# Two contraction tiles instead of one between the short products, in the projections of a three-block transformer kernel

## The chip, the cores and the metric

The kernel runs on one core of one Trainium2 chip. The metric is the device time of one execution in microseconds (us). A core has TensorE (PE in the profile; its weight loads are PEld), VectorE (DVE), ScalarE (ACT), GpSimd (POOL) and SyncE (SP), which here issues most DMAs. Each engine works through its own list of instructions in the order in which the program wrote them.

## The reference, cut to what matters

One batch of 512 tokens, 1024 wide, in float32, goes through two blocks of a first model and one of a second. The change touches the middle one, the gated delta rule, and the last one.

```python
def first_block(x, ...):
    for i in range(2):                                  # block 0: attention, block 1: delta rule
        h = rms_norm(x); mem_n = rms_norm(mem)
        mixed = attention(h, mem_n) if i == 0 else deltanet(h, mem_n)
        x = x + rms_norm(mixed)
        x = x + rms_norm(swiglu(rms_norm(x)))
    return x

def deltanet(h, mem_n):                                 # 6 heads of 128, chunks of 64 tokens
    qkv, z, gate_in, q_mem = split(h @ w_in)            # the projections
    q, k, v = split(silu(conv5(qkv)))                   # q, k are normalised per head
    g, beta = gates(gate_in)                            # for both directions
    o = chunked(q, k, v, g[0], beta[0]) + reversed(chunked)(q, k, v, g[1], beta[1])
    o = rms_norm(o) * out_norm * silu(z)
    return concat([o, memory_attention(q_mem, mem_n)]) @ w_out

def chunked(q, k, v, g, beta):
    # per chunk: solve (I + strict(beta k k^T decay)) [u, w] = [beta v, beta k exp(g)]
    # then, chunk after chunk:
    v_new = u - w @ state
    out = (q * exp(g)) @ state + intra @ v_new
    state = state * exp(g_last) + (k * exp(g_last - g))^T @ v_new

def second_block(x):
    proj = rmsnorm(x) @ w_in                            # the projections again
    mix = concat([gla(proj), s5(proj), nsa(proj)])      # three mixers
    return x + mix @ w_out
```

## The kernel before, in words

**Products.** Every large product is taken in three passes: an operand is split into a high part and a rest, and `mm3` (lines 267 to 269) multiplies rest by high, high by rest, high by high into one PSUM bank. The normalised activations stand transposed in `Xh` and `Xl`: eight contraction tiles of 128 features by 512 tokens. Weights are fetched by SP into `raw` (three buffers), ACT makes the high part `wh` (line 239), DVE the rest `wl` (line 258); four split pieces fit at a time (the set `wsl`).

**Who sets the order.** The program is written by a planner, `Flow`. The parts of the work are generators ("threads") that ask for an engine with an estimated cost, for a buffer from a named set, or for an event. `Flow.run` takes the request that could start first by its own clock; among those of the same engine that could start within 0.1 us of it, it takes the one with the lowest `late` number. So the lists of all engines come out of these estimates; an engine then waits at run time for whatever its next instruction needs. What stands on TensorE between two dependent short products was put there by the planner.

**The projections' thread.** `projector` is used twice: for the delta stage (called in `deltanet`, with the default `late=20`) and for the second block. It goes through weight pieces in a fixed order. A piece of 128 output features is one item; its product is written by `part`, which asks for TensorE once per contraction tile `k` and then writes that tile's three passes. Eight requests make one item, 24 passes (the first four items are taken in two halves of 256 tokens). Items that are lists of pieces (the token-major ones of the second block) have a loop of their own with one request per three passes. In the delta stage the pieces are the gates, then key, query, value of each head, the memory's two query pieces, and z, the output gate, of which heads 3 to 5 stand at the end. When all are written, the event `eP` lets the thread `splits` overwrite `Xh` and `Xl` with the finished heads (lines 1696 and 1698), and the next product begins: the delta block's output projection in `tok_proj`, with the head outputs stationary and `w_out` moving (in the profile `bk<-wh,Xl`, where the projections are `bk<-Xh,wl`). Its first group takes three token tiles through the contraction tiles 6, 7, 0, 1, 2, 3, 4, 5, three passes per token tile and contraction tile: 63 passes that don't need head 5, then 9 that do.

**The short products of a head**, each a thread with a low `late`:
- `key`, `query`, `value`: convolution on DVE (line 1290), transposes (line 1301: `pk`, `pq`, `pv`), `kk` and `kq`;
- `inverse`: transposes of the decayed matrix (line 1469), then five rounds of `x` (line 1502), a transpose `tt` (1483), copies on ACT, `y` (1521), and a predicated copy into `U` on DVE (1526); a last round (1539, 1559) whose results DVE scales into `Uf` (1563);
- `chain`, one per direction, both side by side, four chunks each: `chain<-rhs,Uf` (line 1594), a copy `vn` on ACT (1597), `vs` on DVE (1602), `chain<-vs,ktok` (1604), the new state `St` on DVE (1608 or 1611), `chain<-St,kTh` (1586), `rhs` on DVE (1589), and again; beside it the outputs `o` (1616, 1617);
- `gate_out`: squares on ACT (1641), a power and a multiplication on POOL (1318, 1648), the transpose `poT` (line 1301), and the gated result `oT` on DVE (1651), which `splits` then splits for the output projection.

Of the kernel before, what the change touches and what calls it, by code (L numbers as in the profile page):

```python
# [35 lines left out]
S = 512  # L36
D = 1024
KT = D // P
# [120 lines left out]
class K:  # L159
# [1618 lines left out]
    def projector(self, F, items, eX, eP, late=20, haste=0):  # L1778

        X = self.X
        yield "late", late

        def part(it, t0, t1):
            W, m = it["W"], it["args"][4]
            yield "wait", *eX[t0 // P:t1 // P]  # L1790
            for k in range(KT):
                t = yield "PE", 0.65 * (t1 - t0) / S
                self.mm3(it["p"][:m, t0:t1], (W.h[:, k, :], W.l[:, k, :]), (X.h[:, k, t0:t1], X.l[:, k, t0:t1]),
                         k == 0, k == KT - 1)
            if t1 == S:
                F.put("wsl", t)
                it["done"]["tok"] = t
            return t
        lent = ["px", "lv"]
        for nm in lent:  # L1800
            yield "move", nm, "mm"
        for t0, t1 in ((0, 256), (256, S)):
            for it in items[:4]:
                if not t0:
                    yield "get", "mm"
                    it["p"] = self.psum("mm")
                    yield "wait", it
                t = yield from part(it, t0, t1)
        for i, it in enumerate(items):
            if i < 4:  # L1810
                continue
            if i == len(items) - haste:
                yield "late", -0.5
            if lent:
                yield "move", "mm", lent.pop()
            if isinstance(it, dict):
                yield "wait", it
                yield "get", "mm"
                it["p"] = self.psum("mm")
                t = yield from part(it, 0, S)  # L1820
                continue
            yield "wait", *it, it[0]["use"]
            for u in range(4):
                yield "wait", eX[u]
                yield "get", "mm"
                p = self.psum("mm")
                sl = slice(u * P, (u + 1) * P)
                for k in range(KT):
                    W, kk = it[k // 4]["W"], k % 4
                    t = yield "PE", 0.33  # L1830
                    self.mm3(p[:, :256], (X.h[:, k, sl], X.l[:, k, sl]), (W.h[:, kk, :], W.l[:, kk, :]),
                             k == 0, k == KT - 1)
                evac, late_ = it[0]["use"]["f"]
                F.add(evac(u, p), late_, t)
            for _ in range(2):
                F.put("wsl", t)
        eP["tok"] = t
# [1447 lines left out]
```

## Time and profile before

| what | value |
|---|---|
| three runs of the kernel | 1831.49, 1836.02, 1836.78 us; median 1836.02 |
| the profiled execution | 1834.01 us, span of its profile 1832.3 us |
| TensorE busy | 97% of the span, 12127 matmuls |
| mean granted TensorE clock | 0.991 of full speed |
| chain that ended last | PE 88%, DVE 7%, issue 2%, ACT, DMA, POOL 1% each |

The profile is one execution with every instruction's start and duration. The page gives busy time per engine. The windows view gives it per stretch, with the granted TensorE clock as a share of full speed (1.00 is the level of 2.4 GHz, 0.50 that of 1.2 GHz). The timeline gives single instructions; a matmul's duration there contains its way through the pipeline, so that the distance between two starts, not the duration, is what it costs on a busy TensorE. An entry in square brackets is idle time of the engine just before the instruction, and what ended it.

Places in time: the delta stage's first transposes stand at 708 us, its last projection at 1028 us, `poT` of head 5 at 1054 us; the second block's projections run from 1488 us.

### The profile page before, as it was taken

What the parts mean: (1) busy time and instruction counts of PE and PEld (TensorE: products, weight loads), DVE (VectorE), ACT (ScalarE), POOL (GpSimd) and SP (SyncE); (2) the same over time, 40 slices, a digit from 0 to 9 for tenths busy, and PEclk for the clock granted to TensorE, in tenths of its full rate; (3) what the DMA queues carried; (4) which work ended last, traced back from release to release, by engine and by line L of the source; (5) the groups of instructions that cost most, each with busy time, mean ns of one, the idle gap of its engine ahead of it and who ended that gap; (6) DMA issues with size and microseconds to landing.
All of it is one profiled execution on the core that took longest, in us unless ns stands there. A gap on an engine that the chain in (4) does not pass through costs nothing.

```text
span 1832.3 us, 30457 instructions
## 1 busy us (share of the span) xinstructions
PE 1782.6 (97%) x12127; PEld 1488.2 (81%) x12127; DVE 977.5 (53%) x1997; ACT 769.7 (42%) x1848; POOL 337.3 (18%) x496
## 2 busy tenths in 40 slices
PE   6999999999999999999999989999999999999999
PEld 5988888888888887787878778888888888887787
DVE  6333366423333378775876456454533566466673
ACT  5433445332322245655655445333222352344671
POOL 5200001000000021221222153175450032210000
PEclk8999999999999999999999999999999999999999
DMA  6511113433233233111110155345333252552112
GB/s 187 149 58 49 55 59 127 138 92 103 93 92 104 92 115 81 42 30 36 36 36 25 47 130 137 116 137 145 98 111 102 74 164 80 157 145 67 36 36 81
DMA packets 213006, 167.85 MB, mean 92 GB/s; under 512 B 21996, under 2 KB 185084, under 8 KB 212864
## 3 DMA queue, kind: packets, MB, share of 16 engines
q1 hardware_dynamic: 204832, 154.39, 28.5%
q0 software_dynamic: 4560, 9.42, 2.0%
q10 hardware_dynamic: 3472, 2.10, 0.4%
q8 instruction: 95, 1.56, 0.4%
q14 instruction: 47, 0.39, 0.1%
HBM read 152.23 MB, written 13.65 MB: 91 GB/s over the span
## 4 chain that ended last, share of the span: by engine, by line
PE 88%; DVE 7%; issue 2%; ACT 1%; DMA 1%; POOL 1%; ACTq 0%; SPq 0%; DVEq 0%; POOLq 0%
PE bk L267 23%; PE bk L268 22%; PE bk L269 22%; PE x L1502 2%; PE y L1521 2%; PE no L2739 1%; DVE hn L1290 1%; DVE wl L258 1%; PE npT L2722 1%; PE gs L2095 1%; PE tt L1483 1%; PE ms_s L825 1%; DVE hs L908 1%; PE as L627 1%; PE ns L2708 1%
## 5 line engine op out<-in xcount | busy, mean ns | idle before, releaser
L258 DVE TENSOR_TENSOR wl<-raw,wh 128x512 fp32r<-128x512 f32 x450 | 315.7, 742 | 369.4 <-ACT wh L239 368.7
L239 ACT ACTIVATE wh<-raw 128x512 fp32r<-128x512 f32 x474 | 272.7, 622 | 539.1 <-PE bk L269 304.3
L267 PE MATMUL bk<-Xh,wl 128*128 128x512 f32 (+2 forms) x1312 | 495.0, 377 | 0.2 <-ACT Xh L917 0.2
L268 PE MATMUL bk<-Xl,wh 128*128 128x512 f32 (+2 forms) x1312 | 478.4, 365 | 0.5 <-DVE Xl L922 0.3
L269 PE MATMUL bk<-Xh,wh 128*128 128x512 f32 (+2 forms) x1312 | 478.4, 365 | 0.0
L267 PEld LDWEIGHTS bk<-Xh,wl 128*128 128x128 f32 (+1 forms) x1312 | 247.2, 188 | 41.2 <-issue 5.0
L269 PEld LDWEIGHTS bk<-Xh,wh 128*128 128x128 f32 (+1 forms) x1312 | 247.0, 188 | 40.1
L268 PEld LDWEIGHTS bk<-Xl,wh 128*128 128x128 f32 (+1 forms) x1312 | 247.5, 189 | 34.8 <-DVE Xl L922 0.9
L267 PE MATMUL bk<-wh,Xl 128*128 128x256 f32 (+1 forms) x456 | 167.4, 367 | 6.0 <-ACT wh L239 4.3
L268 PE MATMUL bk<-wl,Xh 128*128 128x256 f32 (+1 forms) x456 | 158.4, 347 | 0.1
L269 PE MATMUL bk<-wh,Xh 128*128 128x256 f32 (+1 forms) x456 | 158.2, 347 | 0.0
L267 PE MATMUL bk<-wh,Al 128*128 128x512 f32 x352 | 139.8, 397 | 0.0
L268 PE MATMUL bk<-wl,Ah 128*128 128x512 f32 x352 | 139.6, 396 | 0.0
L269 PE MATMUL bk<-wh,Ah 128*128 128x512 f32 x352 | 138.6, 394 | 0.0
L887 POOL TENSOR_TENSOR nc<-ncm,nhalf 128x1 f32<-128x1 f32 x16 | 11.6, 723 | 690.1 <-DVE ncm L885 686.0
L267 PEld LDWEIGHTS bk<-wh,Xl 128*128 128x128 f32 x456 | 96.0, 211 | 20.1 <-ACT wh L239 4.7
L269 PEld LDWEIGHTS bk<-wh,Xh 128*128 128x128 f32 x456 | 96.4, 211 | 7.9
L268 PEld LDWEIGHTS bk<-wl,Xh 128*128 128x128 f32 x456 | 96.5, 212 | 7.5 <-DVE wl L258 1.0
L1059 DVE TENSOR_TENSOR sg<-sg,bk 128x512 f32<-128x512 f32 x44 | 30.3, 688 | 124.4 <-PE bk L269 119.9
L269 PEld LDWEIGHTS bk<-wh,Ah 128*128 128x128 f32 x352 | 66.1, 188 | 16.0
L267 PEld LDWEIGHTS bk<-wh,Al 128*128 128x128 f32 x352 | 66.1, 188 | 16.0
L268 PEld LDWEIGHTS bk<-wl,Ah 128*128 128x128 f32 x352 | 66.1, 188 | 15.4
(588 smaller groups left out, 2678.3 us busy)
## 6 DMA issues: line engine op xcount, KB each, us to landing
raw<-in_ffn_w_gate_up_dram SPq DMA_DIRECT2D x88, 512.0 KB, 3.9
raw<-in_ffn_w_down_dram SPq DMA_DIRECT2D x44, 512.0 KB, 3.3
raw<-in_dn_w_in_dram SPq DMA_DIRECT2D x27, 512.0 KB, 3.7
raw<-in_att_w_in_dram SPq DMA_DIRECT2D x20, 512.0 KB, 3.7
raw<-in_w_in_dram SPq DMA_DIRECT2D x20, 512.0 KB, 4.2
raw<-in_mem_w_kv_dram SPq DMA_DIRECT2D x8, 512.0 KB, 3.7
raw<-in_att_w_out_dram SPq DMA_DIRECT2D x8, 512.0 KB, 3.3
xd<-x SPq DMA_DIRECT2D x8, 512.0 KB, 3.2
```

What stands on the lines that cost most here:

```text
L239: nc.scalar.activation(wh[:, sl], ev["raw"][:, sl], AF.Copy)
L258: eng.tensor_tensor(wl[:, sl], raw[:, sl], wh[:, sl].bitcast(F32), op=OP.subtract)
L267: mm(out, A[1], B[0], start=first, stop=False, **kw)
L268: mm(out, A[0], B[1], start=False, stop=False, **kw)
L269: mm(out, A[0], B[0], start=False, stop=last, **kw)
L627: nc.tensor.matmul(s[:, c, lo:hi], qT[rr, c, ts], kT[rr, c, k0 + lo:k0 + hi], start=True, stop=True)
L825: nc.tensor.matmul(s[:, c, :], q[rr, c, ts], self.memK[i][rr, c, :], start=True, stop=True)
L908: nc.vector.scalar_tensor_tensor(hh[:, hv[i]], x[:, t, hv[i]], r2, r["gain"][:, hv[i]], op0=OP.mult, op1=OP.mult)
L1059: nc.vector.tensor_tensor(sg, sg, pu, op=OP.mult)
L1290: nc.vector.scalar_tensor_tensor(acc[:, d0:d1], raw[:, d0 + o:d1 + o], cw[:, ti, tap:tap + 1], acc[:, d0:d1], op0=OP.mult, op1=OP.add)
L1502: nc.tensor.matmul(dn8(x)[HB[c % 2], d, c // 2, :], Ln[d][HB[f], c, HB[f]], U[HB[f], d, c, :], start=True, stop=True)
L1521: nc.tensor.matmul(dn8(y)[HB[f], d, n, :], T[HB[par], d, n, f, :], xs[f][HB[par], d, n, :], start=True, stop=True)
```

## The change

In `part`, one request now covers two contraction tiles, at twice the estimated cost, and writes six passes. Nothing is added or removed; the planner then orders the instructions of all engines anew. Line numbers above 1788 grow by one.

```diff
         def part(it, t0, t1):
             W, m = it["W"], it["args"][4]
             yield "wait", *eX[t0 // P:t1 // P]
-            for k in range(KT):
-                t = yield "PE", 0.65 * (t1 - t0) / S
-                self.mm3(it["p"][:m, t0:t1], (W.h[:, k, :], W.l[:, k, :]), (X.h[:, k, t0:t1], X.l[:, k, t0:t1]),
-                         k == 0, k == KT - 1)
+            for k0 in range(0, KT, 2):
+                t = yield "PE", 1.3 * (t1 - t0) / S
+                for k in (k0, k0 + 1):
+                    self.mm3(it["p"][:m, t0:t1], (W.h[:, k, :], W.l[:, k, :]), (X.h[:, k, t0:t1], X.l[:, k, t0:t1]),
+                             k == 0, k == KT - 1)
             if t1 == S:
                 F.put("wsl", t)
                 it["done"]["tok"] = t
```

**TensorE, the short products of head 0 early in the delta stage** (transposes `pq` and `pkT`, then the rows of the decay). The piece of the difference:

```order
 L268 MATMUL bk<-Xl,wh 128x512
 L269 MATMUL bk<-Xh,wh 128x512
+L267 MATMUL bk<-Xh,wl 128x512
+L268 MATMUL bk<-Xl,wh 128x512
+L269 MATMUL bk<-Xh,wh 128x512
 L1301 MATMUL pq<-ident,qTh 128x128 x4
-L267 MATMUL bk<-Xh,wl 128x512
-L268 MATMUL bk<-Xl,wh 128x512
-L269 MATMUL bk<-Xh,wh 128x512
 L1301 MATMUL pkT<-ident,ktok 128x128 x4
```

Three passes that stood between the two transposes have joined the burst ahead of them, and the transposes now stand side by side.

**TensorE, the end of head 4's inverse** (its last `y`) and the start of its chain. Before:

```order
L1559 MATMUL y_9214<-xs_9152,T 64x64 x4
L267 MATMUL bk<-Xh,wl 128x512
L268 MATMUL bk<-Xl,wh 128x512
L269 MATMUL bk<-Xh,wh 128x512
L1411 MATMUL kq<-qTh,kTh 128x128 x4
L1594 MATMUL chain<-vtok,Uf 128x128
L267 MATMUL bk<-Xh,wl 128x512
```

Now:

```order
L269 MATMUL bk<-Xh,wh 128x512
L1559 MATMUL y_9385<-xs_9327,T 64x64 x4
L1594 MATMUL chain<-vtok,Uf 128x128 x2
L1604 MATMUL chain<-vs_9409,ktok 128x128
L1604 MATMUL chain<-vs_9412,ktok 128x128
L1617 MATMUL o<-vn_9405,AT_8426 128x128
L1469 MATMUL y_9423<-ident,Ln_9224 128x128 x4
L1586 MATMUL chain<-St_9419,kTh 128x128
```

The last pass of the delta stage's 528 now stands ahead of head 4's last `y`; before, 72 passes still followed the chain's first product. Nothing stands any more between that `y`, the chain's first product and its second.

**TensorE, the end of head 5's chain, up to `poT`.** Before (between the last of these rows and `poT` follow the other `o` products and 24 passes of the output projection):

```order
L1586 MATMUL chain<-St_9935,kTh 128x128
L1586 MATMUL chain<-St_9940,kTh 128x128
L267 MATMUL bk<-wh,Xl 128x512
L268 MATMUL bk<-wl,Xh 128x512
L269 MATMUL bk<-wh,Xh 128x512
L1594 MATMUL chain<-rhs_9949,Uf 128x128
L1594 MATMUL chain<-rhs_9954,Uf 128x128
L267 MATMUL bk<-wh,Xl 128x512
L268 MATMUL bk<-wl,Xh 128x512
L269 MATMUL bk<-wh,Xh 128x512
L1616 MATMUL o<-St_9935,qe_9011 128x128
L1617 MATMUL o<-vn_9958,AT_8972 128x128
```

Now:

```order
L1586 MATMUL chain<-St_9974,kTh 128x128
L1586 MATMUL chain<-St_9979,kTh 128x128
L1594 MATMUL chain<-rhs_9988,Uf 128x128
L1594 MATMUL chain<-rhs_9990,Uf 128x128
L1616 MATMUL o<-St_9974,qe_9165 128x128
L1617 MATMUL o<-vn_9994,AT_9146 128x128
L1616 MATMUL o<-St_9979,qe_9345 128x128
L1617 MATMUL o<-vn_9996,AT_9319 128x128
L1301 MATMUL poT<-ident,otok 128x128 x4
L267 MATMUL bk<-wh,Xl 128x512
```

No pass of the output projection stands between head 5's first chain product and its `poT` any more: all 63 that don't need head 5 stand ahead of it (54 stood ahead of `poT` before), and the first pass behind `poT` is one that does need head 5.

Counted in the two orders from the first transpose of line 1301 in the delta stage to `poT` of head 5, the passes come in 116 bursts before (75 of three, 25 of six, 16 longer) and in 93 now (10 of three, 76 of six, 7 longer).

## Rows read from the trace of the kernel before

**Rows 1.** The page: busy time per engine, share of the span, instructions.

```profile
PE 1782.6 (97%) x12127; PEld 1488.2 (81%) x12127; DVE 977.5 (53%) x1997; ACT 769.7 (42%) x1848; POOL 337.3 (18%) x496
```

**Rows 2.** Windows: stretch, length, busy us (PE, PEld, DVE, ACT, POOL), PE clock, DMA.

```profile
708.00:1028.00 320.00, 313.09 (x3544) 255.91 (x3544) 224.32 (x512) 174.95 (x500) 68.95 (x57) 0.99 0.13 38
1028.00:1056.90 28.90, 25.75 (x153) 21.61 (x151) 15.33 (x40) 10.60 (x32) 6.45 (x9) 0.94 0.11 37
...
1490.00:1690.00 200.00, 195.82 (x1700) 167.38 (x1700) 118.36 (x270) 81.02 (x188) 39.22 (x44) 0.99 0.44 120
```

**Rows 3.** Timeline of TensorE, one burst of six: start, duration, instruction.

```profile
742.26 0.48 PE L267 MATMUL bk<-Xh,wl 128*128 128x512 f32 x1
742.58 0.40 PE L268 MATMUL bk<-Xl,wh 128*128 128x512 f32 x1
...
743.50 0.39 PE L269 MATMUL bk<-Xh,wh 128*128 128x512 f32 x1
743.82 0.97 PE L1521 MATMUL y<-xs,T 64*64 64x64 f32 x32
```

**Rows 4.** TensorE's waits, 708 to 1060 us: total, times, longest.

```profile
PE chain L1604 <- DVE vs L1602: 2.8, 2, 1.6
PE chain L1594 <- DVE Uf L1563: 2.1, 2, 1.7
PE x L1502 <- DVE U L1526: 1.8, 1, 1.8
PE x L1502 <- DVE U L1472: 1.2, 1, 1.2
```

**Rows 5.** Timeline of TensorE in head 5's chain and behind it.

```profile
1033.57 1.05 PE L1604 MATMUL chain<-vs,ktok 128*128 128x128 f32 x4
...
1037.90 0.60 PE L1594 MATMUL chain<-rhs,Uf 128*128 128x128 f32 x4
...
1039.72 0.61 PE L1604 MATMUL chain<-vs,ktok 128*128 128x128 f32 x4
1040.09 0.48 PE L267 MATMUL bk<-wh,Xl 128*128 128x512 f32 x1
...
1041.75 0.61 PE L1586 MATMUL chain<-St,kTh 128*128 128x128 f32 x4
...
1042.90 0.60 PE L1594 MATMUL chain<-rhs,Uf 128*128 128x128 f32 x4
...
1048.42 0.39 PE L1617 MATMUL o<-vn,AT 128*128 128x128 f32 x2
...
1054.11 0.60 PE L1301 MATMUL poT<-ident,otok 128*128 128x128 f32 x4
...
1056.94 0.50 PE L267 MATMUL bk<-wh,Xl 128*128 128x512 f32 x1 [0.17 <-DVE Xl L1698]
```

**Rows 6.** Timeline of DVE and POOL in the same stretch.

```profile
1038.68 0.51 DVE L1602 TENSOR_SCALAR vs<-vn,ksc 128x128 f32<-128x128 f32 x2 [0.30 <-ACT vn L1597]
1039.43 0.69 DVE L1698 TENSOR_TENSOR Xl<-oT,Xh 128x512 fp32r<-128x512 f32 x1 [0.23 <-ACT Xh L1696]
1040.14 0.60 DVE L1608 SCALAR_TENSOR_TENSOR St<-St,etot,chain 128x128 f32<-128x128 f32 x2
...
1042.18 0.61 DVE L1589 SCALAR_TENSOR_TENSOR rhs<-chain,neg,vtok 128x128 f32<-128x128 f32 x2 [0.83 <-PE chain L1586]
...
1052.08 1.04 POOL L1648 TENSOR_TENSOR otok<-otok,rro 128x512 f32<-128x512 f32 x1
```

**Rows 7.** Windows around two stretches with waits, same columns.

```profile
733.00:745.00 12.00, 9.06 (x160) 7.59 (x160) 11.72 (x24) 9.09 (x19) 3.45 (x3) 1.00 0.17 45
...
1073.00:1078.00 5.00, 4.90 (x11) 3.60 (x12) 2.12 (x5) 1.25 (x4) 0.00 (x0) 0.51 0.57 151
```

**Rows 8.** TensorE's two longest waits, 1490 to 1832 us.

```profile
PE ncs L2649 <- DVE Q L2617: 2.0, 2, 1.6
PE nqT L2609 <- DVE nqd L2604: 1.9, 1, 1.9
```

## The prediction

> **What bounds the kernel now.** I read the page first: TensorE is busy for 1782.6 us of the span [rows 1], so what can be won or lost is its idle time and the price of its busy time. The windows give the idle time by stage [rows 2]: 320.00 - 313.09 = 6.9 us between the first transposes of the delta stage and its last projection, 28.90 - 25.75 = 3.15 us from there to the first product that needs head 5's result, 4.2 us in the second block's projections. The stages ahead of the delta stage aren't touched; in the second feed-forward the order stays as it is. The view of waits names what ended the idle time: always DVE, with a result of a head's convolution, inverse or chain that came late [rows 4]. The timeline then shows the price of the bursts [rows 3] and, at the end of the delta stage, the steps of a chain with and without passes between them [rows 5, 6].
>
> **The change part by part.** No instruction comes or goes, no DMA moves past another one of its queue. What counts is where passes stand.
>
> *Bursts.* Inside a burst a pass costs 0.23 us ((743.50 - 742.58) / 4). The first one costs 0.32 (742.26 to 742.58), and the last one 0.32 up to the short product behind it [rows 3]. So a burst costs 0.18 us beyond its passes. The delta stage has 93 in place of 116. Where a burst goes, two short products meet and have an edge of their own, so I take three quarters: 23 x 0.13 = **-3.0 us** (bounds 0 and 23 x 0.18 = -4.1). The second block has as many bursts as before.
> The Trainium skill says on the page "TensorE: Matmul & The Clock Gate", section "Step-by-step: what each phase is for", that TensorE pulls weight loads ahead of matmuls in flight, so that the next tile's weights load while this one runs. By that rule changing over would be free and this term 0; the trace doesn't agree, with 0.32 against 0.23 at both ends of the burst.
>
> *Waits in the body of the delta stage.* 6.9 us, most of it in four waits of 1.2 to 1.8 us, two of the inverse and two of the chain [rows 2, 4]. Where a dependent short product follows a burst, the burst is now three passes longer and hides 0.7 us more; where a burst has gone, it hides 0.7 less. DVE's own order is new too, and which of its results comes late can't be read. I take **-2.0 us**: 0.7 of three of the four waits. Bounds: -6.9 (all hidden) and +3 (the four places at which a burst has gone from behind a short product, 0.7 each).
>
> *The end of the delta stage.* Twice the passes go into each gap, so the projections are used up earlier, ahead of head 4's chain. From there the planner fills gaps from the output projection, three passes at a time, and all 63 that it may take are used up before head 5's chain begins. That chain had a burst at nearly every step and has none now. Its steps cost:
> - chain product to `vs` to next product: from 1037.90 to the first half of `vs` (1038.68 + 0.26) and 0.1 to start: 1.1 us [rows 5, 6]. TensorE's own four instructions fill 0.37 (1039.72 to 1040.09); 0.73 is idle.
> - `chain<-St` to `rhs` to next product: 1041.75 to 1042.18 + 0.30 and 0.07: 0.80, less 0.37: 0.43 idle.
> - in between, the state `St` (1039.72 to 1040.14 + 0.30) is hidden by the output products.
> - three chunks: 3 x (0.73 + 0.43) = 3.5; the last chunk 0.2; the wait for `Uf` at the start 0.5 (2.1 for two of them where DVE was busy with other work [rows 4]).
> - the last `o` to `poT`: squares, power, multiplication end at 1052.08 + 1.04 = 1053.12, 4.7 us after 1048.42; less 0.2 of its own: 4.5 idle. 24 passes hid this before.
> - `poT` to the first pass with head 5: 1054.11 to 1056.94, 2.83, less 0.37: 2.45 idle. Nine passes hid it but for 0.17.
>
> Together 3.5 + 0.2 + 0.5 + 4.5 + 2.45 = 11.15, less the 3.15 that this stretch idled before: **+8.0 us**. Bounds +5 (the steps that pair up hide each other) and +11.
>
> *Head 4's chain* starts without cover for its first two steps: 0.5 + 0.73. The seven splits for the output projection (0.69 each on DVE [rows 6]) now fall between its steps in place of head 5's. Fully exposed they are 4.8; about 2 should show, since bursts of three still stand at half of the steps. **+3.2 us** (bounds +1.2 and +6.0).
>
> *The clock.* After the wait that ends at 1073 us, 11 passes took 4.90 us at a granted clock of 0.51 [rows 7], 0.445 each in place of 0.23: 2.4 lost. The idle time around `poT` should bring the same. Before, the chain's first round ran slowly too: 1033.57 to 1037.90 is 4.33, the next round 3.18 with two more pairs of output products (0.4) [rows 5]; so 1.6 lost goes. Net **+0.8 us**. Bounds -1.6 and +5.
>
> *The second block.* Its two longest waits, 1.9 and 2.0 us [rows 8], have more ahead of them now: 39 passes of half width where 27 stood (12 x 0.12 = 1.4) and 12 of full width where 9 stood (0.7). **-2.0 us**; bounds -4 (both gone) and +3 (four steps of the last mixer without a burst of three).
>
> The stall at 1073 us is a chain of its own from the first pass with head 5 to weights that are fetched when a buffer comes free, and moves along with it: 0.
>
> Sum: -3.0 - 2.0 + 8.0 + 3.2 + 0.8 - 2.0 = **+5.0 us** on the profiled execution's 1834.0. The median of the three runs shown is 2.0 above that execution, so I put the time at 1836.0 + 5.0 = **1841.0 us**.
>
> **The rivals.**
> *The tail runs at 1.2 GHz.* For: head 5's chain idles 1.16 of some 3.2 us in each chunk, and after the waits around 1029 to 1033 us the chain's round was slow [rows 5]. Against: the stretch from 733 to 745 us idled 3 of 12 us and kept a clock of 1.00 [rows 7]. It decides where the idle share lies between these two. The price: three groups of 0.37 in a chunk take twice as long, 1.1, for four chunks of head 5 and perhaps one of head 4: 5.5 us. Time 1841.0 + 5.5 = 1846.5.
> The Trainium skill has the same page's section "What's actually happening" for it: "the default state is throttled, and activity releases the throttle"; by that rule sparse small products are what brings the lower level back. The two stretches just named show both outcomes.
>
> *The waits on DVE vanish* (not slower). Place: the waits of the body and the two of the second block, all for results of DVE that were a little late. If the longer bursts hide all of them and head 4 shows its bare 1.2, the sum is -3.0 - 6.9 + 8.0 + 1.2 + 0.8 - 4.0 = -3.9: 1832.1. It needs two bursts' worth of extra cover (1.4 us) at most of these places. For: each wait is below 1.9 us. Against: DVE was busy for 11.72 of 12 us at the first of them [rows 7], so that there its own work sets the time.
>
> *Changing over is free*, as the rule on weight loads has it: the sum without -3.0 is +8.0, 1844.0. Rows 3 speak against it.
>
> That the change doesn't do what it says is excluded: the new order has 76 bursts of six.
>
> **How the numbers follow.** About 0.3%, 5.5 us, is what a measurement of this kernel can tell from no change: below 1830.5 is faster, above 1841.5 slower. My sum lies just at the upper edge. Forecast: 0.49, of which 0.25 slower and 0.24 within. Tail at the low clock: 0.20, all slower. Waits vanish: 0.25, of which 0.12 faster and 0.13 within. Free changes: 0.06, of which 0.05 slower. So slower 0.50, same 0.38, faster 0.12. The range takes in both rivals' times and the larger bounds of the tail: 1830 to 1850. Sums above 0.3% and sums within it share most of the chance but sit beside each other; the forecast's own range is 1835 to 1847.
>
> **What would show it.** The profile of the changed kernel should show TensorE idle for 9 to 14 us between the last projection of the delta stage and the first pass with head 5 (3.15 before), among it one wait of 4 to 5 us ahead of `poT`, ended by POOL, and one of about 2.4 behind it, ended by DVE's split; a granted clock of 0.5 after them; below 6.9 us of idle time in the body; and the two waits of the second block shorter by 1 us or so each. I am wrong if the gap ahead of `poT` is missing, if the body's idle time grows, or if the second block's last mixer, which I left out but for a bound, begins to wait.

## The result, and the profile after

The changed kernel took 1850.96 us (median of five runs, 1846.61 to 1855.85), the kernel before 1835.06 us beside it (1831.49 to 1836.78): a ratio of 1.0088, 95% interval 1.0075 to 1.0101. It is slower, as forecast, but by 15.9 us in place of 5.0, and just outside the range. The profiled execution is the one of 1846.61 us, 12.6 above that of before.

The page's engine line of the changed kernel answers to [rows 1]: the same 12127 matmuls, 9.2 us more of busy time.

```profile
PE 1791.8 (97%) x12127; PEld 1493.8 (81%) x12127; DVE 979.1 (53%) x1997; ACT 767.9 (42%) x1848; POOL 338.0 (18%) x496
```

Windows of the changed kernel, columns as in [rows 2]: the delta stage to its last projection, head 4's chain, head 5's chain to the first pass that needs it; then, in the second block, 3.9 us of short products and what followed them.

```profile
707.00:1003.70 296.70, 289.93 (x3094) 238.37 (x3095) 210.10 (x471) 162.36 (x462) 63.03 (x51) 0.99 0.14 40
1003.70:1047.00 43.30, 41.96 (x527) 34.13 (x525) 19.94 (x53) 16.40 (x48) 6.02 (x7) 0.96 0.04 14
1047.00:1067.40 20.40, 11.71 (x81) 9.65 (x75) 8.61 (x28) 5.01 (x21) 5.44 (x8) 0.87 0.08 27
...
1532.70:1536.60 3.90, 3.90 (x56) 3.63 (x54) 1.69 (x5) 0.63 (x1) 0.51 (x1) 1.00 0.16 32
...
1536.60:1550.30 13.70, 13.70 (x82) 11.11 (x81) 5.24 (x13) 3.09 (x6) 3.29 (x7) 0.50 0.33 99
```

The last two lines are the surprise. TensorE is busy all the time, no wait stands ahead, and for 13.7 us the granted clock is 0.50. The kernel before ran the same short products, and much the same passes behind them, at 1.00, as its windows show:

```profile
1527.70:1531.35 3.65, 3.65 (x54) 3.38 (x53) 1.55 (x5) 0.63 (x1) 0.30 (x1) 1.00 0.12 18
1531.35:1544.00 12.65, 12.65 (x136) 10.29 (x135) 7.52 (x20) 3.47 (x7) 3.50 (x7) 1.00 0.39 108
```

TensorE's waits in the changed kernel, 707 to 1070 us and then 1490 to 1844 us (total, times, longest); they answer to [rows 4, 8]. The wait ahead of `poT` is there, and a wait of the second block that before did not have: `s5y`, a product of the S5 mixer, for its state `q` from DVE. The wait for `npT`, in the block's last mixer, was 0.3 us before.

```profile
PE pk L1301 <- DVE kraw L1271: 5.1, 2, 3.8
PE poT L1301 <- POOL otok L1648: 4.4, 1, 4.4
PE mo L864 <- DVE mpT L854: 2.5, 1, 2.5
PE chain L1604 <- DVE vs L1602: 2.5, 4, 1.1
PE bk L267 <- DVE Xl L1698: 2.2, 1, 2.2
...
PE nqT L2610 <- DVE nqd L2605: 3.1, 2, 1.8
PE npT L2723 <- ACT nP L2715: 1.4, 2, 1.1
PE s5y L2333 <- DVE q L2314: 1.4, 1, 1.4
```

TensorE's timeline in head 5's chain, changed kernel; it answers to [rows 5].

```profile
1047.86 0.61 PE L1594 MATMUL chain<-vtok,Uf 128*128 128x128 f32 x4
1048.93 0.71 PE L1604 MATMUL chain<-vs,ktok 128*128 128x128 f32 x4 [0.47 <-DVE vs L1602]
...
1050.76 0.75 PE L1594 MATMUL chain<-rhs,Uf 128*128 128x128 f32 x4 [0.22 <-DVE rhs L1589]
...
1064.06 1.12 PE L1301 MATMUL poT<-ident,otok 128*128 128x128 f32 x4 [4.36 <-POOL otok L1648]
1067.41 0.80 PE L267 MATMUL bk<-wh,Xl 128*128 128x512 f32 x1 [2.23 <-DVE Xl L1698]
```

### The profile page after: what moved, and what is told of

It is laid out like the page before. It is cut to its first block, busy times and chain, and to the rows that moved or that the text cites. A ratio compares the mean times of both kernels' runs of the same rounds, so it can differ in the third digit from the quotient of the medians.

```text
span 1844.9 us, 30450 instructions
## 1 busy us (share of the span) xinstructions
PE 1791.8 (97%) x12127; PEld 1493.8 (81%) x12127; DVE 979.1 (53%) x1997; ACT 767.9 (42%) x1848; POOL 338.0 (18%) x496
## 4 chain that ended last, share of the span: by engine, by line
PE 88%; DVE 7%; ACT 2%; issue 2%; POOL 1%; DMA 1%; ACTq 0%; DVEq 0%; POOLq 0%
PE bk L267 23%; PE bk L268 22%; PE bk L269 22%; PE y L1521 1%; PE x L1502 1%; DVE wl L258 1%; PE no L2740 1%; DVE hn L1290 1%; PE npT L2723 1%; PE gs L2096 1%; PE ms_s L825 1%; PE tt L1483 1%; PE as L627 1%; DVE hs L908 1%; PE hT L915 1%
## 5 line engine op out<-in xcount | busy, mean ns | idle before, releaser
L258 DVE TENSOR_TENSOR wl<-raw,wh 128x512 fp32r<-128x512 f32 x450 | 320.3, 753 | 363.9 <-ACT wh L239 363.2
```

Of the source, the lines that this page charges most:

```text
L258: eng.tensor_tensor(wl[:, sl], raw[:, sl], wh[:, sl].bitcast(F32), op=OP.subtract)
```

## The experiments

They ran on three chips (e1 to e4, e5 to e8, e9 to e12), each time beside the kernel before, whose median was 1833.95, 1835.77 and 1834.96 us there; each ratio is to that. All start from the kernel before, with the number of contraction tiles per request as a parameter `n` of `projector`, a function of the item's place (27 items in the delta stage):

```diff
+            for k0 in range(0, KT, n):
+                t = yield "PE", 0.65 * n * (t1 - t0) / S
+                for k in range(k0, k0 + n):
+                    self.mm3(...)
```

### One block at a time

The delta stage alone (e1, the first pair of lines), the second block alone (e2, the second pair):

```diff
-        F.add(self.projector(F, order, eX, eP))
+        F.add(self.projector(F, order, eX, eP, n=lambda i: 2))
...
-        F.add(self.projector(F, W["order"], eX, eAll, haste=1))
+        F.add(self.projector(F, W["order"], eX, eAll, haste=1, n=lambda i: 2))
```

> Two tiles per request in the delta stage only; the second block keeps one. Theory A (the cost is the delta stage's end: no passes left between the steps of head 5's chain, plus the low clock behind it; in the second block's first mixers the changed kernel's profile fell to the low clock by chance of where the clock's decision fell, not by its order): about +7 us against the kernel before, 1842. Theory B (each block's new order costs in its own place): also about +7 here, so this run alone doesn't tell them apart; its sum with the next one does. Theory C (the longer bursts cost nothing by themselves, all of it is the low clock): the same idle time as before at the end of the delta stage and a lower clock.

> Two tiles per request in the second block only. Theory A: within 3 us of the kernel before on average, 1833 to 1838, with the profile either free of a low-clock stretch around the first mixers or with one that the kernel before can have too. Theory B: +6 to +8 us, 1841 to 1843, and the low-clock stretch of some 14 us around the first mixers is there again.

Measured: e1 1840.24 us, ratio 1.0035 (1.0018 to 1.0052), 12 runs from 1834.1 to 1848.8; e2 1836.06 us, ratio 1.0004 (0.9985 to 1.0022), 12 runs from 1834.12 to 1844.72. The halves don't add: +0.35% and +0.04% against +0.88% for both. Theory A's forecasts came nearly (+6.3 and +2.1 us), theory B's +6 to +8 for e2 did not; but then about half of what the change costs stands in neither half. e2's profile (1844.11 us) shows the low clock too: 20.5 us at 0.50 from 1558.1 us on, behind a wait of 1.40 us for `q`. And runs of one kernel differ by up to 15 us, with a mean clock of 0.984 in the longest and 0.995 in the shortest. Even the kernel before does that: of the 29 runs shared by this and the next section, 21 lie from 1830.6 to 1835.7 and eight from 1837.9 to 1844.9. So something that comes in some executions alone is at work, and more often with the change: nine of its eleven runs (five above, six of e4 below) took 1846.6 us or more.

### Two tiles for the first heads alone, and the change once more

```diff
+        F.add(self.projector(F, order, eX, eP, n=lambda i: 2 if i < 15 else 1))
```

This leaves 36 passes of the output projection beside head 5's chain (54 before, none in the change). The second block is that of before.

> Two tiles per request in the delta stage for the first 15 pieces (gates, heads 0 to 2, memory) and one for the other 12 (heads 3 to 5 and their z). 36 passes of the output projection then stand between the steps of head 5's chain and poT, where the kernel before has 54 and the changed one none, but only 3 of them behind the last o, where the kernel before has 24. Theory A: the chain's own steps are covered, the wait ahead of poT stays at 3.5 to 4 us: +3 us against the kernel before, 1838. Theory B: about as much as with two tiles in the whole delta stage, +7.

> The changed kernel once more, for a second trace. Theory A: the wait ahead of poT (4.4 us) and behind it (2.2 us) stand in it again; the low-clock stretch around the first mixers of the second block may be missing or lie elsewhere, and the time of the profiled execution then differs from the first one's by about 6 us. Theory B: the stretch is there again, of the same length. Median 1847 to 1853 by both.

Measured: e3 1835.06 us, ratio 0.9995 (0.9975 to 1.0015), in two groups, 1827.4 to 1832.8 and 1837.3 to 1841.1; e4 1850.89 us, ratio 1.0084 (1.0051 to 1.0118), from 1840.6 to 1859.4. e3 can't be told from the kernel before, so the forecasts of both theories (+3 and +7) missed. The profile of e3 fell into its upper group, and its windows show the low clock at the same place, for longer, though its second block is in the order of before:

```profile
1525.10:1528.80 3.70, 3.70 (x55) 3.43 (x53) 1.60 (x5) 0.63 (x1) 0.32 (x1) 1.00 0.13 21
1528.80:1552.70 23.90, 23.90 (x148) 18.92 (x149) 7.88 (x21) 3.47 (x7) 3.48 (x7) 0.50 0.30 91
```

Half of 23.9 us would be 12 us; from the first to the last `gs` product it is 75.2 us here and 64.6 in the kernel before, so the stretch costs some 11 us. e4's profile (1857.44 us) has two such stretches, one of 13.7 us at the first place, as in the change's first profile, and one behind the wait for `q`. Its timeline at that wait, and the window behind:

```profile
1569.27 0.66 PE L2333 MATMUL s5y<-q,wB 128*128 128x64 f32 x4 [1.37 <-DVE q L2314]
...
1572.00:1592.50 20.50, 20.50 (x159) 16.73 (x158) 7.65 (x16) 3.21 (x11) 4.04 (x4) 0.50 0.36 109
```

In the change's first profile the same wait stands, and the clock stays at 1.00 behind it:

```profile
1567.57 0.66 PE L2333 MATMUL s5y<-q,wB 128*128 128x64 f32 x4 [1.37 <-DVE q L2314]
...
1550.30:1700.00 149.70, 144.33 (x1203) 122.29 (x1203) 91.14 (x208) 57.45 (x148) 26.55 (x25) 1.00 0.43 118
```

So there are two places in the second block where the clock can fall: a run of products of 64 columns (`s5y`, `gs`, `sl`) without a projection pass between them, and the wait for `q`. If the low clock there is a large part of what the change costs, work put into these places that does nothing else should make the kernel faster.

### Redundant passes into the two places

```diff
+    def fill(self, dst, n):
+        X = self.X.h[:, 0, :]
+        for _ in range(n):
+            self.nc.tensor.matmul(dst, X[:, :P], X[:, :dst.shape[-1]], start=True, stop=True)
...
+                    if q < 2:
+                        self.fill(spare, 3)                 # ahead of s5y; 12 at e == 2 in e9, e10, e12
...
+                    if q in (1, 2):
+                        for v in range(2):
+                            self.fill(bank[:, v * 256 + 128 * (e % 2):v * 256 + 128 * (e % 2) + 128], 2)
```

Nothing is left out; `spare` is the unused half of the bank, and what is written over `bank` is overwritten by the products of `sl`. In e8, e10 and e11 the same helper writes 16 or 13 passes of 512 columns into `poT`'s bank ahead of head 5's transposes:

```diff
+            p = yield from tok(ot.rearrange("p c k -> p (c k)"), "poT", 16 * (h == 5))
```

> The change, with 12 redundant matmuls of 256 columns and 16 of 128 columns (bf16-like f32 passes of a row tile that is at hand, written into the bank before its own products overwrite it) ahead of the first two groups of s5y products and of two groups of sl products of the second block; nothing is left out. By the 0.23 us of a 128x512 pass they cost 2.3 us of TensorE. Theory A (most of what the change costs beyond the idle time is a stretch at 1.2 GHz that begins where the second block emits only short s5y, gs and sl products): no row of clock below 0.6 lasts longer than 3.4 us between 1500 and 1650 us, and the time falls from 1851 us in spite of the added work, to 1842 to 1845. Theory B (the second block's new order costs by its own waits, the clock is a bystander): 1853 us, 2 us above the change. Theory C (the whole of it is lost at the end of the delta stage, and the second block costs nothing): 1853 too, and the stretches at 1.2 GHz in the second block go without a gain.

> The kernel before with the same added matmuls. Its runs so far lie at 1830.6 to 1835.7 us (21) and at 1837.9 to 1844.9 us (8). Theory A: the upper group is what the stretch at 1.2 GHz costs, so it goes; all runs within 4 us of one another, at 1833 to 1837 (2.3 us above the lower group), the median between no change and +0.1%. Theory B and C: the two groups stay, both 2 us higher, median 1837 or above.

> Two row tiles at a time for the first 15 pieces of the delta stage alone, one for its last 12 and in the second block, with the same added matmuls. Without them its runs lay at 1827 to 1833 and 1837 to 1841 us. Theory A: one group, 1830 to 1834, faster than before by 0.1 to 0.25%. Theory B and C: both groups 2 us higher, median 1837.

> As e5, and 16 further redundant 128x512 passes (3.6 us) ahead of the transposes of head 5's gated output (poT), where the changed kernel's TensorE waits 4.36 us. Theory A (that wait costs twice: its idle time, which is lost either way, and the 10.24 us at 1.2 GHz behind it): poT starts no later than in e5, the stretch at 1.2 GHz behind it is gone or 3.4 us, and the time is 4 to 5 us below e5's. Rival D (the low clock there comes from the short products of head 5's chain ahead of it, or from the 2.23 us wait behind poT): the stretch stays, the time is e5's within 1 us.

Measured: e5 1857.59 us, ratio 1.0113 (1.0098 to 1.0129), all runs 1856.1 to 1858.4; e6 1836.80 us, 1.0005 (0.9995 to 1.0014), all runs 1835.5 to 1838.4; e7 1833.98 us, 0.9991 (0.9980 to 1.0002), 1830.9 to 1838.4; e8 1853.36 us, 1.0085 (1.0055 to 1.0115), 1841.9 to 1859.5. The kernel before took 1830.7 to 1841.2 beside them.

e6 came as theory A says: all runs within 3 us, against 10 of the kernel before beside it, and the median pays 1 us for it. The times alone are weak evidence, since only one of those 24 runs of the kernel before lay above 1839 us. e7's median is at the upper edge of theory A's range, but half of its runs lie above 1834, up to 1838.4, so it is not the one group that was forecast. The profiles say more. None of the eight with added matmuls (e5 to e12) has a stretch at the first place; of the six without, three have it (the change twice, and e3). e7's windows, to be held against e3's, show the short products thinned with added matmuls and the clock at 1.00 behind them, with 250 matmuls in the time in which e3 did 148:

```profile
1522.99:1528.80 5.81, 5.81 (x80) 5.27 (x80) 1.98 (x5) 0.63 (x1) 0.89 (x2) 1.00 0.17 42
1528.80:1552.70 23.90, 23.90 (x250) 18.67 (x249) 15.72 (x39) 6.39 (x12) 6.49 (x9) 1.00 0.28 85
```

e5 missed theory A's range by 12.6 us. The first stretch is gone from its profile, but the wait for `q` is still there, 1.03 us, and behind it stands the longest stretch of all. Timeline and window of e5:

```profile
1564.47 0.66 PE L2340 MATMUL s5y<-q,wB 128*128 128x64 f32 x4 [1.03 <-DVE q L2318]
...
1565.20:1596.00 30.80, 30.80 (x237) 26.13 (x236) 8.06 (x20) 5.88 (x20) 4.20 (x4) 0.50 0.32 95
```

That left two readings: the wait brings the clock down, or the short products around it do. The next runs put nine more matmuls ahead of the group that waits, so that they take up the time of the wait.

> As e5, with 12 redundant matmuls of 256 columns (3 in e5) ahead of the group of s5y products whose second half waits for q (1.40 us in the change run again, 1.03 us in e5): they take the place of that wait. Theory A (the stretch at 1.2 GHz of 30.7 us in e5 begins because TensorE stands there): no row of clock below 0.6 longer than 3.4 us in the second block; the added work falls into the wait, so the time is that of the undisturbed runs of the change (1840.7) and the 2.3 us of e5, 1842 to 1846, all runs within 4 us. Theory B (the new order of the second block costs by its waits, not by the clock): 1857 us, as e5. Rival E (it is the short gs products between the passes, not the wait, that bring the clock down): the stretch begins a little before or behind the same place, 1855 us or more.

> As e9, with the 16 passes of e8 ahead of poT as well. Theory A: all runs at the level of the two lowest of e8, 1840 to 1844 us, 3 to 5 us under e9; this is the change with its clock at 2.4 GHz in nearly all places, and what is left over before (some 7 us) is idle time and 2.3 us of added work. Rivals B and E: 1853 us, spread over 15 us, as e8.

> Two row tiles at a time in the second block alone, with the added matmuls of e9. The same matmuls cost the kernel before about 1 us in e6 (1836.8 us). Theory A (what the second block's order costs is the clock behind the wait for q, and its waits cost 2 us): 1836 to 1839 us, one group, against 1834 to 1845 without the added work. Theory B (the order costs 6 us by its waits): 1842 us.

Measured: e9 1844.07 us, ratio 1.0043 (1.0026 to 1.0060), 1840.8 to 1846.8; e10 1843.47 us, 1.0047 (1.0030 to 1.0064), 1840.4 to 1850.1; e12 1838.42 us, 1.0015 (0.9997 to 1.0033), 1836.3 to 1842.4. The medians of e9 and e12 lie in theory A's ranges, but their runs spread over 6 us. e12 is not faster than e2: in the second block alone the added matmuls cost the median about what they save. e9 differs from e5 by nine matmuls of 256 columns and is 13.5 us faster. e5's four runs alone could mislead, but e8 and e10 differ at this place in the same way: of the eleven runs of e5 and e8 nine took 1852 us or more, and none of the seventeen of e9 and e10 took more than 1850.1. e9's timeline at the place, and the window that answers to e5's:

```profile
1561.43 0.43 PE L2338 MATMUL s5y<-uj,wB 128*128 128x64 f32 x2
1561.84 0.66 PE L2340 MATMUL s5y<-q,wB 128*128 128x64 f32 x4
...
1565.00:1596.00 31.00, 31.00 (x351) 25.59 (x350) 11.78 (x31) 8.83 (x30) 7.09 (x7) 1.00 0.46 140
```

The wait is gone and the clock stays at 1.00, 351 matmuls where e5 did 237. That decides against theory B, and against rival E as it was put: with more work in it, the change costs 9 us in place of 16. It does not separate the wait from the short products around it, since the nine matmuls end the idle time and also put wide products among narrow ones. What the second block's order costs without the low clock is read from its first `gs` to the end of the profile: 328.7 us in e9 (1511.8 to 1840.5) and 328.8 in e12 (1507.5 to 1836.3), against 325.6 in e7 (1504.1 to 1829.8), which has the order of before, nine added matmuls fewer and no low clock either. e6 has the same second block as e7 and took 326.9, but 3.4 us of that ran at 0.50, near 1642 us. Of the 3 us up to 1 is the nine matmuls (half of 0.23 us each, an estimate), so the order costs 2 to 3 us.

In e8 and e10 the passes ahead of `poT` do what was expected of them there: the wait ahead of it falls from 4.36 to 0.71 us, the stretch of 10.24 us at 1.2 GHz behind `poT` is gone although the wait of 2.23 us behind it stays, and rival D falls. But e10's median is 0.6 us under e9's, not 3 to 5, and four of its nine runs lie above the 1844 that was forecast; with such spreads 0.6 us is no difference. (e8's 4.2 under e5 tells little of this place: two of its seven runs, 1841.9 and 1842.7 with a mean clock of 0.994, seem to have escaped the stretch behind `q`, and in its profile that stretch was 23.9 us, and 30.7 in e5.) The profiles of e9 and e10 differ by luck as well: e9's lacks a stretch of 3.4 us near 1008 us that the change and e10 have, so its head 5 began 1.5 us earlier, and its stretch behind `poT` was 6.8 us. A second reason is in three timelines, of SP, ACT and TensorE. A piece of the output weights is fetched only after passes with head 5 have run. The kernel before:

```profile
1062.66 0.38 SPq L203 DMA_DIRECT2D raw<-in_dn_w_out_dram  x1
...
1072.41 1.15 ACT L239 ACTIVATE wh<-raw 128x512 fp32r<-128x512 f32 x2 [6.91 <-DMA raw<-in_dn_w_out_dram]
...
1073.10 0.79 PE L267 MATMUL bk<-wh,Xl 128*128 128x512 f32 x1 [4.30 <-ACT wh L239]
```

e9:

```profile
1073.35 0.38 SPq L203 DMA_DIRECT2D raw<-in_dn_w_out_dram  x1
...
1080.11 1.15 ACT L239 ACTIVATE wh<-raw 128x512 fp32r<-128x512 f32 x2 [3.92 <-DMA raw<-in_dn_w_out_dram]
...
1080.79 0.50 PE L267 MATMUL bk<-wh,Xl 128*128 128x512 f32 x1 [1.30 <-ACT wh L239]
```

e10:

```profile
1064.21 0.66 PE L1302 MATMUL poT<-ident,otok 128*128 128x128 f32 x4 [0.71 <-POOL otok L1649]
...
1072.82 0.38 SPq L203 DMA_DIRECT2D raw<-in_dn_w_out_dram  x1
...
1079.88 1.15 ACT L239 ACTIVATE wh<-raw 128x512 fp32r<-128x512 f32 x2 [4.22 <-DMA raw<-in_dn_w_out_dram]
...
1080.56 0.50 PE L267 MATMUL bk<-wh,Xl 128*128 128x512 f32 x1 [1.60 <-ACT wh L239]
```

The fetch took 9.75 us before (1062.66 to 1072.41), 6.8 in e9 and 7.1 in e10. TensorE waits for it in all three. With the clock high it arrives earlier and waits longer: 1.60 us in e10, 0.51 in the change's first profile. So about 1.1 of the 3.1 us (half of the busy 6.2 us in that stretch, an estimate) are lost there.

### A version that is faster than both

e3's delta stage, three added matmuls ahead of each half of the first `s5y` group and half of those ahead of `sl`, and 13 passes ahead of `poT`.

> Two row tiles at a time for the first 15 pieces of the delta stage alone, with the added matmuls ahead of one group of s5y and one of sl products (1.1 us, half of e7's) and 13 redundant 128x512 passes (2.9 us) ahead of poT, where TensorE stands 3.66 us in e7. Theory A: the 6.8 us at 1.2 GHz behind poT go (3.4 us), 1.1 us of added work go, but the passes behind reach the wait for weights at 1073 us the earlier, which takes up to 3 us of it back: 1830 to 1833 us, faster than before by 0.15 to 0.3%. Rival D (the low clock behind poT does not hang on its wait): 1833, as e7.

Measured: 1830.14 us (1828.9 to 1836.6, 12 runs), ratio 0.9970 (0.9957 to 0.9984), 0.3% faster than before and in theory A's range. Windows: the body, head 5's chain, the output projection behind it, and the second block from its first `gs`.

```profile
707.00:1035.50 328.50, 320.66 (x3588) 261.78 (x3589) 231.94 (x526) 179.70 (x510) 69.27 (x57) 0.99 0.14 38
1035.50:1058.20 22.70, 19.77 (x123) 16.79 (x121) 7.96 (x26) 5.18 (x21) 5.00 (x8) 1.00 0.08 25
1058.20:1080.30 22.10, 21.48 (x85) 16.78 (x85) 11.34 (x20) 10.12 (x24) 11.13 (x17) 0.92 0.89 231
1502.80:1826.80 324.00, 315.96 (x2610) 261.12 (x2609) 190.10 (x425) 146.65 (x390) 37.47 (x40) 1.00 0.30 87
```

The head's end stays covered by 36 passes and the fill, and the wait for weights at 1073 us, 4.30 before, is 0.22 here. In the profiles the gain is the delta stage's: the first `gs` stands at 1502.8 us, 5.2 earlier than before, and from there to the end it is 324.0 us, 324.2 before.

## Why the prediction was right in its direction and wrong in its size

The sum was +7.0 us for the delta stage and -2.0 for the second block. The first transpose of line 915 behind the delta block's output projection stands at 1084.9 us before and at 1090.7 now: **+5.8**, or +6.9 from the stage's own first transpose, which stands 1.1 us earlier now. So the delta stage as a whole came out right, but by luck: its terms missed by up to 5 us in both directions, as listed below. From the first `gs` to the end the profile has 324.2 us before and 331.8 now: **+7.6**, where I had -2.0. **The step that failed is the second block's term**, in its sign and above all in leaving out the clock, which I had priced for the delta stage alone (+0.8, bounds -1.6 and +5).

Windows from the first `gs` to the end, columns as in [rows 2]: the kernel before, the change, the change again (e4), e6, e9.

```profile
1508.10:1832.30 324.20, 315.80 (x2596) 261.08 (x2595) 190.10 (x425) 146.50 (x390) 37.46 (x40) 0.99 0.31 87
1513.10:1844.90 331.80, 321.22 (x2596) 264.11 (x2595) 194.11 (x427) 146.05 (x390) 38.54 (x40) 0.98 0.30 85
1514.80:1855.70 340.90, 330.30 (x2596) 271.24 (x2595) 194.21 (x427) 146.16 (x390) 38.60 (x40) 0.95 0.30 83
...
1508.70:1835.60 326.90, 318.96 (x2624) 264.45 (x2623) 190.61 (x425) 146.39 (x390) 36.94 (x40) 0.99 0.30 86
...
1511.80:1840.50 328.70, 319.51 (x2633) 263.75 (x2632) 193.31 (x427) 146.00 (x390) 38.55 (x40) 1.00 0.30 86
```

- *The second block (-2.0).* The wait for `nqT` rose from 1.9 to 3.1 us and that for `npT` from 0.3 to 1.4 (the last mixer's, another sign of being wrong that I had named), that for `ncs` (2.0) went, and the wait for `q` came: idle time is 10.6 us where it was 8.4. The order costs 2 to 3 us (e9 and e12 against e7), and the rest is the low clock: 13.7 us of it lose 6.8, and a stretch of 3.4 us that the profile of before has near 1638 us lost 1.7 there, 5.1 net. In e4's (340.9 us) the two stretches lose 17.1. The median of all runs is probably higher than the profiled execution for the same reason: those that took longer have a lower mean clock (0.983 at 1855.85 us, 0.988 at 1846.61). My search for waits could not find the first place, since no wait stands there.
- *The body: bursts (-3.0), waits (-2.0), head 4 (+3.2), together -1.8.* From the first transpose to the first product of head 5's chain it is 321.3 us with 528 passes before and 340.9 with 591 now. Less 0.227 for each pass and half of the stretches at 1.2 GHz (3.4 us before, 10.2 now, which is 3.4 us lost in addition, and which no term of the sum had): 199.7 and 201.6, **+1.9**. Idle time there did not fall (7.36 and 8.12 us), which I had named as a sign of being wrong. Where passes went from between two short products, some of the waits between them showed; the saving at the edges of the bursts, if there was one, is covered by that and was not measured by itself. Head 4's part of the idle time is 1.34 us (43.30 - 41.96), not 3.2.
- *The end (+8.0).* From the first product of head 5's chain to the first pass that needs it, less the passes: 27.6 - 63 x 0.227 = 13.3 before, 19.5 now: **+6.3**. The clock works the other way here: 3.4 us of this stretch ran at 1.2 GHz before, all busy (1.7 lost), and 5.2 us do now, of which TensorE stands still for 4.1 (0.6 lost). Without it the end costs +7.4. The steps were the ones I named: 0.47 and 0.22 shown idle per chunk (0.73 and 0.43 forecast), 4.36 ahead of `poT` (4.5), 2.23 behind (2.45).
- *The stall at 1073 us (0).* It didn't move along unchanged: from the first pass with head 5 to the end of the wait for weights it is 16.2 us before and 14.7 now, as the fetch took less, **-1.5**; and the 6.8 us at 1.2 GHz that began in the 4.30 us wait are missing now, **-3.2** up to the first transpose of line 915. With the chain's start 1.1 us earlier: 1.9 + 3.4 + 6.3 - 1.5 - 3.2 - 1.1 = 5.8.
- *The rivals.* The tail did not run at 1.2 GHz: head 5's chain kept the upper level up to 1062.2, in the wait ahead of `poT`. The 10.24 us at the lower level from there on have a net price of 1.7 us: e10, without them, needs 41.1 us from the start of head 5's chain to that transpose, the change 42.8. The waits on DVE did not vanish. That changing over is free can't be ruled out: without the -3.0 for the bursts the body's terms give +1.2, nearer to the +1.9 measured, and no run isolates what fewer edges save. Why the body gained nothing is the weaker part of this account: no run separates its terms.

What the Trainium skill says on the page "TensorE: Matmul & The Clock Gate", section "What's actually happening", that "activity releases the throttle", fits e9 against e5 and e7 against e3, where more work kept the clock up. Once down, though, the clock stayed at 0.50 through 13.7 to 30.7 us in which TensorE was never idle; there the measurement doesn't fit it.

Still open: what decides whether an execution falls into a stretch or not, and whether at the second place it is the idle time or the short products. The same kernel does both, and the change moved the first place by 5 us; whether it was the time of arrival that made the stretches more frequent wasn't tried.

## What to carry to other kernels

When a change bunches large passes, list the places where they went away, also those without a wait: a few microseconds of small products alone were followed by 14 to 24 us at half the clock. Such a place is cheap to test, with redundant passes in an idle or thin stretch (3.3 us of them in e9 made the change 7 us faster), and one profile isn't enough to judge it, since some executions have the stretch and some don't. And the last dependent chain of a stage needs its cover kept for it: a limit on how early the filler may be used (e3 in place of e1) was worth 5 us here, and longer bursts with that limit (e3) were no faster than before.

## What was not expected of the hardware

TensorE's granted clock fell to 0.50 with no idle time ahead of it, behind 3.7 to 3.9 us of products of 64 columns, in some executions and not in others; it fell behind waits of 1.03 and 1.37 us as well, and behind another of 1.37 us it did not. It then stayed for 13.7, 20.5, 23.9 and 30.7 us, while passes of 128x256 and 128x512 ran with short products among them and TensorE was never idle. In the kernel before too, runs of 1838 to 1845 us with a mean clock of 0.986 to 0.991 stand beside runs of 1831 to 1836 with 0.990 to 0.994, and with added matmuls at the two places (e6) all its runs came within 3 us.
